# A planner that sets the order of emission counts every result as ready a fixed small reserve later than its clocks say

## The chip, the cores and the metric

One Trainium2 chip, one core. The metric is the device time of one execution in microseconds (us). Most executions of this kernel agree within about 0.3%. Engines: PE (TensorE, matmuls), DVE (VectorE), ACT (ScalarE), POOL (GpSimd), SP (SyncE, here only DMA issue).

## The reference, cut to what matters

T = 512 positions, D = 1024 channels, everything float32.

```python
h = rmsnorm(x, g_mix)
z = h @ w_in                         # conv 2048, q 1024, k 1024, v 1024, gates 2048 columns
y_conv = silu(layernorm(causal_conv_31(a * sigmoid(gate)))) @ w_conv_pw
q, k = partial_rope(q), partial_rope(k)          # 8 heads x 2 parts x 64
# differential attention, causal, per block of 128 queries:
p = softmax(mask(q k^T / 8)); attn = p[part 0] - lam * p[part 1]; o = attn @ v
y_attn = (rmsnorm(o, g_subln) * (1 - lambda_init)) @ w_attn_pw
x = x + (gate_conv * y_conv + gate_attn * y_attn) @ w_out
h2 = rmsnorm(x, g_ffn)
x = x + (silu(h2 @ w_ffn_gate) * (h2 @ w_ffn_up)) @ w_ffn_down     # d_ff = 2816
out = rmsnorm(x, g_final)
```

## The kernel before

**Arithmetic and tiling.** The block is kept transposed, channels on the 128 partitions and the 512 positions along the free axis. Each float32 operand of a dense product is split in a high part (fp32r) and a low rest (fp32r), and a product is three matmuls: high by high, high by low, low by high. Weights come as units of 128x1024 (512 KB each, one DMA on SP's queue into `wr`, 3 buffers). `next_unit` keeps the splitting some units ahead of their use: ACT casts a unit to `wh` (4 buffers), and the rest `wl = wr - wh` (4 buffers) is made on POOL in four pieces of 128x256 for units 3 to 63, on DVE for the others.

**Stages, with their times from the start of the span.** Loading x and its norm, to about 31 us; eight chunks of the convolution branch (`chunkA`, two units and 48 matmuls each), to about 101; eight heads, to about 325 (for each pair of heads `project_v` makes V from two units, then every head has one chunk for q and k); eight chunks of gates, to about 401; four chunks of the attention's output projection, to about 448; then the convolution's projection, `w_out`, the FFN, and a tail, to 908.5.

**Work that is slipped between the dense matmuls.** Generators ("tasks") hold it. `softmaxes(h)` splits q and k of a head (tiles T and `kz`), makes scores (a pair of matmuls for each block of queries and part, called S00, S01, S10, ... here: block, then part), the exponentials and the difference of the two parts. `outputs(h)` transposes that difference (the turns T0, T1, T2: matmuls `at<-ident,T`), splits the result on ACT and DVE, and multiplies it by V (P.V: `at<-T,T`). `head_norm` normalises the heads' outputs during the gate chunks: their reciprocal roots come from one POOL instruction on the tile `oc`. `conv_norm` is the layernorm of the convolution during the attention projection: column sums on PE, a small scaling on DVE (`sm`), a power on POOL (`rc`), four diagonal tiles on DVE (`dg`), a broadcast by PE (`cv<-dg,ones`). `norm_x` and `norm_ffn` have the same shape. The convolution's 31 taps for each channel tile (DVE, `cv<-T,vec_sb,cv`, 248 in all) are filler: `pump` puts one into DVE's queue whenever DVE's planned clock is behind PE's, or before a DVE instruction that would wait. When a channel tile's last tap is emitted, an add onto `csum` (128x512) is put into POOL's queue.

**What sets the order.** Each engine runs its queue in the order of emission, and that order comes from a planner, `class Model` (lines 78 to 125). It keeps a planned clock for each engine (`clk`), and for each tile a planned `ready` time. Every operation recorded (helper line L142, so that nearly all instructions have this line) advances its engine's clock by an assumed cost and sets

```python
for n in outs:
    self.ready[n], self.writer[n] = end + self.LAT[eng] + self.SLACK, eng
```

where LAT is the assumed latency of a hop (PE 0.2, DVE 0.14, ACT 0.145, POOL 0.075, DMA 0.13). `start` takes the latest of the engine's clock and the ready times of what an operation reads and writes, except that PE does not wait for PE. `alloc`, which gives a tile a buffer of its ring, uses the last use of the old tile + 0.13, without SLACK.

`need(tiles)` is the latest ready time of some tiles. A task yields the time that it needs, and is resumed by `service` once that time is due:

```python
def service(until=0.0):
    while True:
        now[0] = max(clk["pe"], until)
        due = [t for t in tasks if t[0] <= now[0]]
```

The dense work calls `service` through `run`, before each three matmuls:

```python
yield need(hi, lo, outs[c], *mov[k])        # chunkA; project_v: need(hi, lo, ps)
```

So `until` is the ready time of what the next dense matmul takes, its own accumulator `outs[c]` among it. That accumulator was last written by PE, with ready time PE's clock + 0.2 + SLACK: a task is thus resumed if it is due within that much of PE's clock.

Of the kernel before, what the change touches and what calls it, by code (L numbers as in the profile page):

```python
# [80 lines left out]
class Model:  # L81


    LAT = {"pe": 0.2, "dve": 0.14, "act": 0.145, "pool": 0.075, "dma": 0.13}
    SLACK = 0.0

    def __init__(self):
        self.clk = {"pe": 0.0, "dve": 0.0, "act": 0.0, "pool": 0.0, "dma": 2.2}
# [21 lines left out]
    def op(self, eng, cost, ins, outs):  # L110
# [5 lines left out]
        for n in outs:  # L116
            self.ready[n], self.writer[n] = end + self.LAT[eng] + self.SLACK, eng

# [945 lines left out]
```

## Time and profile before

| | us |
|---|---|
| runs | 908.42, 910.53, 911.55 (median 910.53) |
| the profiled execution | 910.34 |
| its span | 908.5 (1.84 lie outside the span) |
| PE busy | 886.2 (98% of the span), 4246 matmuls |
| DVE, ACT, POOL busy | 567.8, 373.6, 293.5 |
| chain that ended last | PE 53% and no other engine by 1% |

PE is the engine that never rests for long, so a change can gain only what PE loses in waits. In the rows further below a bracket as `[0.34 <-DVE T L142]` means that the engine stood idle for 0.34 us before this instruction, and that a tile T written by DVE ended the idle time. Matmuls of a row overlap in their pipeline: their starts lie closer than their durations say.

### The profile page before, as it was taken

The page shows a single profiled execution, that of the slowest core. Times are in us where ns is not written, and L with a number is a line of the kernel's source. Part 1 is how long each engine was busy: PE and PEld are TensorE (multiplying, and loading weights), DVE is VectorE, ACT ScalarE, POOL GpSimd, SP SyncE. Part 2 cuts the span into 40 slices and gives each one's busy share as a digit, 9 for nine tenths or more (in the row PEclk, how much of TensorE's full clock was granted, in tenths as well). Part 3 has the DMA queues.
Part 4 walks back from the last instruction along what each step waited for, and adds up shares of the span by engine and source line. Part 5 has one row for each costly group of instructions (what it writes and reads, how often), then busy time and mean ns, then how long its engine had stood idle before and what let it go on. Part 6 is the DMA issues. An engine that isn't in the chain of part 4 may idle for free.

```text
span 908.5 us, 11288 instructions
## 1 busy us (share of the span) xinstructions
PE 886.2 (98%) x4246; PEld 733.1 (81%) x4246; DVE 567.8 (63%) x952; ACT 373.6 (41%) x615; POOL 293.5 (32%) x369
## 2 busy tenths in 40 slices
PE   8989999999999999999999999999999999999996
PEld 6868888888887777688888888888888888888886
DVE  6699899898989889957455553343433433422422
ACT  7332336665657884445322343322232222312212
POOL 2755577683938456455100001111111111000000
PEclk9999999999999999999999999999999999999999
DMA  8222222121121122233323441233332222332302
GB/s 278 93 71 95 91 93 94 48 93 47 66 70 51 70 70 71 78 108 93 105 81 130 147 142 64 76 102 107 100 105 97 93 93 92 116 102 84 116 24 93
DMA packets 26151, 85.20 MB, mean 94 GB/s; under 512 B 3040, under 2 KB 3808, under 8 KB 26096
## 3 DMA queue, kind: packets, MB, share of 16 engines
q1 hardware_dynamic: 24944, 82.52, 27.6%
q10 hardware_dynamic: 1152, 1.97, 0.6%
q8 instruction: 33, 0.54, 0.2%
q14 instruction: 22, 0.18, 0.1%
HBM read 82.38 MB, written 2.10 MB: 93 GB/s over the span
## 4 chain that ended last, share of the span: by engine, by line
PE 53%; DVE 0%; issue 0%; POOL 0%; ACT 0%; POOLq 0%
PE mm L142 27%; PE at L142 22%; PE cv L142 4%; DVE dg L142 0%; DVE T L142 0%; POOL rc L142 0%; ACT T L142 0%; POOLq L196 0%; POOL sm L142 0%; DVE fs L142 0%
## 5 line engine op out<-in xcount | busy, mean ns | idle before, releaser
L142 PE MATMUL mm<-T,wh 128*128 128x512 f32 x1360 | 426.6, 395 | 4.0 <-DVE T L142 3.2
L142 PEld LDWEIGHTS mm<-T,wh 128*128 128x128 f32 x1360 | 251.3, 189 | 58.7 <-DVE T L142 4.2
L142 PE MATMUL mm<-T,wl 128*128 128x512 f32 x680 | 266.2, 391 | 0.5 <-DVE wl L142 0.5
L142 POOL TENSOR_TENSOR wl<-wr,wh 128x256 fp32r<-128x256 f32 x244 | 189.4, 809 | 153.9 <-ACT wh L142 153.9
L142 ACT CAST wh<-wr 128x1024 fp32r<-128x1024 f32 (+1 forms) x148 | 148.9, 1033 | 78.6 <-PE mm L142 38.7
L142 POOL TENSOR_TENSOR T<-T,T 128x256 f32<-128x256 f32 (+1 forms) x96 | 90.1, 949 | 231.0 <-DVE T L142 211.2
L142 DVE SCALAR_TENSOR_TENSOR cv<-T,vec_sb,cv 128x512 f32<-128x512 f32 x232 | 160.7, 747 | 0.1
L142 PE MATMUL at<-T,wh 128*128 128x512 f32 x496 | 154.0, 392 | 0.0
L142 PEld LDWEIGHTS mm<-T,wl 128*128 128x128 f32 x680 | 128.2, 189 | 28.4 <-DVE wl L142 1.0
L142 DVE TENSOR_TENSOR wl<-wr,wh 128x1024 fp32r<-128x1024 f32 (+1 forms) x88 | 101.9, 1186 | 69.8 <-ACT wh L142 69.2
L142 ACT CAST T<-T 128x512 fp32r<-128x512 f32 (+2 forms) x112 | 67.9, 618 | 139.0 <-POOL T L142 85.2
L142 DVE TENSOR_TENSOR T<-T,T 128x512 fp32r<-128x512 f32 (+2 forms) x111 | 86.1, 777 | 58.5 <-ACT T L142 56.6
L142 PEld LDWEIGHTS at<-T,wh 128*128 128x128 f32 x496 | 93.6, 189 | 19.5
L142 DVE TENSOR_TENSOR T<-mm,T 128x512 f32<-128x512 f32 (+1 forms) x76 | 51.8, 683 | 85.1 <-PE mm L142 76.7
L142 PE MATMUL mm<-wh,T 128*128 128x256 f32 (+1 forms) x432 | 101.0, 317 | 0.0
L142 PE MATMUL at<-T,wl 128*128 128x512 f32 x248 | 97.0, 391 | 0.0
L142 ACT ACTIVATE T<-T 128x512 f32<-128x512 f32 (+1 forms) x66 | 40.4, 621 | 122.7 <-DVE T L142 122.6
L142 DVE TENSOR_TENSOR T<-at,T 128x512 f32<-128x512 f32 (+4 forms) x59 | 38.0, 649 | 66.9 <-PE at L142 55.3
L142 ACT ACTIVATE T<-T,sm 128x128 f32<-128x128 f32 (+3 forms) x100 | 56.1, 562 | 53.6 <-DVE sm L142 50.1
L142 PEld LDWEIGHTS mm<-wh,T 128*128 128x128 f32 x432 | 73.1, 190 | 5.4
L142 PE MATMUL mm<-wl,T 128*128 128x256 f32 (+1 forms) x216 | 68.2, 316 | 0.0
L142 PEld LDWEIGHTS at<-T,wl 128*128 128x128 f32 x248 | 46.8, 189 | 9.8
(88 smaller groups left out, 649.2 us busy)
## 6 DMA issues: line engine op xcount, KB each, us to landing
wr<-wall SPq DMA_DIRECT2D x145, 512.0 KB, 3.3
T<-xT SPq DMA_DIRECT2D x16, 256.0 KB, 4.4
out<-T ACTq DMA_DIRECT2D x4, 256.0 KB, 2.8
out<-T SPq DMA_DIRECT2D x4, 256.0 KB, 2.6
wr<-wall SPq DMA_DIRECT2D x4, 128.0 KB, 4.2
T<-cs ACTq DMA_DIRECT2D x2, 256.0 KB, 4.7
T<-gfin SPq DMA_DIRECT2D x2, 256.0 KB, 5.1
T<-mask ACTq DMA_DIRECT2D x1, 256.0 KB, 5.0
```

What stands on the lines that cost most here:

```text
L142: r = f(*args, **kw)
```

## The change

One constant of the planner:

```diff
 class Model:
     LAT = {"pe": 0.2, "dve": 0.14, "act": 0.145, "pool": 0.075, "dma": 0.13}
-    SLACK = 0.0
+    SLACK = 0.15
```

Every operation's results, and every load's (`load` goes through `op`), now count as ready 0.15 us later. The engines' planned clocks move only where an operation is planned to wait. No instruction is added or taken away: 4246 matmuls, 952 DVE, 615 ACT and 369 POOL instructions as before. What changes is the order in each queue, at three places as follows (tile names carry a running number, which differs between the two).

PE, the queue around the first scores of head 3, S00, S01, S10, S11 (`at` tiles from T and `kz`), and a turn of head 2 (`at<-ident,T`); `mm` are dense matmuls. Before (S00 stands nine dense matmuls ahead of the first row):

```order
L142 MATMUL at_2147<-T_386_2060,T_384_2058 128x128
L142 MATMUL at_2147<-kz_157,T_384_2058 128x128
L142 MATMUL at_2164<-T_385_2059,T_383_2057 128x256
L142 MATMUL at_2164<-kz_156,T_383_2057 128x256
L142 MATMUL mm_2111<-wh_1869,T_93_504 128x256
L142 MATMUL mm_2111<-wl_1871,T_93_504 128x256
L142 MATMUL mm_2111<-wh_1869,T_94_506 128x256
L142 MATMUL at_2103<-ident,T_351_1939 128x128
L142 MATMUL at_2103<-ident,T_371_2002 128x128
L142 MATMUL at_2103<-ident,T_351_1939 128x128
L142 MATMUL at_2103<-ident,T_371_2002 128x128
L142 MATMUL mm_2111<-wh_1869,T_98_523 128x256
```

After:

```order
L142 MATMUL at_2222<-T_376_2061,T_374_2059 128x128
L142 MATMUL at_2222<-kz_156,T_374_2059 128x128
L142 MATMUL at_2229<-T_377_2062,T_375_2060 128x128
L142 MATMUL at_2229<-kz_157,T_375_2060 128x128
L142 MATMUL at_2237<-T_376_2061,T_374_2059 128x256
L142 MATMUL at_2237<-kz_156,T_374_2059 128x256
L142 MATMUL at_2220<-ident,T_363_2016 128x128
L142 MATMUL at_2220<-ident,T_380_2083 128x128
L142 MATMUL at_2220<-ident,T_363_2016 128x128
L142 MATMUL at_2220<-ident,T_380_2083 128x128
L142 MATMUL at_2244<-T_377_2062,T_375_2060 128x256
L142 MATMUL at_2244<-kz_157,T_375_2060 128x256
```

The first scores moved from the V projection of heads 4 and 5 (mm of 256 columns) into the q and k chunk behind it; S00, S01, S10 and S11 and the turn now follow each other with no dense matmul between.

POOL, the rests of the two weight units of that same V projection (`wl`, four pieces each), and the rotation of q and k (T 128x256) behind them. Before:

```order
L142 TENSOR_TENSOR wl_1786<-wr_1565,wh_1784 128x256 x4
L142 TENSOR_TENSOR wl_1871<-wr_1687,wh_1869 128x256 x4
L142 TENSOR_TENSOR T_152_916<-T_152_916,T_347_1921 128x512
L142 TENSOR_TENSOR T_346_1920<-T_346_1920,T_2_99 128x256
L142 TENSOR_TENSOR T_348_1925<-T_348_1925,T_346_1920 128x256
```

After:

```order
L142 TENSOR_TENSOR wl_1745<-wr_1561,wh_1743 128x256 x4
L142 TENSOR_TENSOR T_152_916<-T_152_916,T_320_1808 128x512
L142 TENSOR_TENSOR wl_1840<-wr_1612,wh_1838 128x256 x4
L142 TENSOR_TENSOR T_325_1857<-T_325_1857,T_2_99 128x256
L142 TENSOR_TENSOR T_326_1859<-T_326_1859,T_325_1857 128x256
```

The add onto `csum` (128x512) moved from behind the two units to between them.

POOL, the power of `head_norm` (`oc`) among the rests of the gates' weight units. Before:

```order
L142 TENSOR_TENSOR wl_3649<-wr_3505,wh_3647 128x256 x4
L142 TENSOR_TENSOR wl_3712<-wr_3558,wh_3710 128x256 x4
L142 TENSOR_TENSOR wl_3782<-wr_3645,wh_3780 128x256 x4
L142 TENSOR_TENSOR oc_988<-oc_988,mhalf 128x32
L142 TENSOR_TENSOR wl_3848<-wr_3708,wh_3846 128x256 x4
```

After:

```order
L142 TENSOR_TENSOR wl_3798<-wr_3645,wh_3796 128x256 x4
L142 TENSOR_TENSOR wl_3867<-wr_3731,wh_3865 128x256 x4
L142 TENSOR_TENSOR wl_3919<-wr_3794,wh_3917 128x256 x4
L142 TENSOR_TENSOR oc_990<-oc_990,mhalf 128x32
L142 TENSOR_TENSOR wl_3979<-wr_3863,wh_3977 128x256 x4
```

`oc` moved three weight units later in POOL's queue (51 units stand ahead of it, against 48).

## Rows read from the trace of the kernel before

**Rows 1.** Windows: stretch, its us, busy of PE PEld DVE ACT POOL, clock, DMA.

```profile
125.00:350.00 225.00, 217.35 (x1207) 182.86 (x1206) 205.54 (x456) 148.74 (x311) 143.01 (x181) 1.00 0.21 69
400.00:425.00 25.00, 24.64 (x113) 19.96 (x112) 17.81 (x29) 14.48 (x20) 13.73 (x18) 1.00 0.34 104
425.00:900.00 475.00, 475.00 (x2173) 395.30 (x2172) 197.34 (x238) 142.09 (x189) 38.70 (x34) 1.00 0.30 98
```

**Rows 2.** Waits of PE, 125 to 350 us: total us, times, longest.

```profile
PE at L142 <- DVE T L142: 2.7, 8, 0.7
PE at L142 <- DVE kz L142: 2.3, 7, 0.6
PE at L142 <- ACT T L142: 1.6, 4, 0.5
PE at L142 <- DVE sm L142: 1.0, 3, 0.6
```

**Rows 3.** Timeline of PE from 203.2 us: start, us, instruction, [idle before <- releaser].

```profile
203.22 0.28 PE L142 MATMUL mm<-wl,T 128*128 128x256 f32 x1
203.34 0.28 PE L142 MATMUL mm<-wh,T 128*128 128x256 f32 x1
203.96 0.30 PE L142 MATMUL at<-T,T 128*128 128x128 f32 x1 [0.34 <-DVE T L142]
204.59 0.33 PE L142 MATMUL at<-kz,T 128*128 128x128 f32 x1 [0.33 <-DVE kz L142]
```

**Rows 4.** The chain of waits: one chunk of 48 dense matmuls (start, us, what).

```profile
459.19 10.88 PE at L142 x48
```

**Rows 5.** Timeline of PE: the last P.V of the attention.

```profile
322.44 1.04 PE L142 MATMUL at<-T,T 128*128 128x256 f32 x6 [0.36 <-ACT T L142]
```

**Rows 6.** Timeline of DVE, 201.4 to 204.6 us.

```profile
201.44 0.68 DVE L142 TENSOR_TENSOR kz<-T,T 64x512 fp32r<-64x512 f32 x1
202.15 1.67 DVE L142 TENSOR_TENSOR T<-T,T 64x512 fp32r<-64x512 f32 x1
203.84 0.69 DVE L142 TENSOR_TENSOR kz<-T,T 64x512 fp32r<-64x512 f32 x1
```

**Rows 7.** Timeline of POOL, 179 to 206 us.

```profile
184.50 3.11 POOL L142 TENSOR_TENSOR wl<-wr,wh 128x256 fp32r<-128x256 f32 x4 [0.84 <-ACT wh L142]
187.56 7.46 POOL L142 TENSOR_TENSOR T<-T,T 128x512 f32<-128x512 f32 x9
...
201.60 1.66 POOL L142 TENSOR_TENSOR T<-T,T 128x512 f32<-128x512 f32 x1 [0.22 <-DVE T L142]
```

**Rows 8.** Timeline of PE: the second unit of that V projection begins.

```profile
193.49 0.40 PE L142 MATMUL mm<-wh,T 128*128 128x256 f32 x2
```

**Rows 9.** Timeline of POOL, 349 to 372 us: `oc` and two units behind it.

```profile
354.91 5.45 POOL L142 TENSOR_TENSOR oc<-oc,mhalf 128x32 f32<-128x32 f32 x1 [1.39 <-DVE gsub L142]
360.33 5.60 POOL L142 TENSOR_TENSOR wl<-wr,wh 128x256 fp32r<-128x256 f32 x8
```

**Rows 10.** Timeline of POOL, 395 to 450 us.

```profile
398.78 1.29 POOL L142 TENSOR_TENSOR T<-T,T 128x512 f32<-128x512 f32 x1
...
413.20 2.81 POOL L142 TENSOR_TENSOR wl<-wr,wh 128x256 fp32r<-128x256 f32 x4 [1.58 <-ACT wh L142]
415.97 1.02 POOL L142 TENSOR_TENSOR rc<-sm,mhalf 128x4 f32<-128x4 f32 x1
```

**Rows 11.** Timeline of DVE, 410 to 420 us: what `rc` takes, what takes it.

```profile
414.39 0.16 DVE L142 TENSOR_SCALAR sm<-at 128x4 f32<-128x4 f32 x1 [0.77 <-PE at L142]
417.02 2.82 DVE L142 TENSOR_SCALAR dg<-ident,rc 128x128 f32<-128x128 f32 x4 [2.47 <-POOL rc L142]
```

**Rows 12.** Timeline of PE: the broadcast of `conv_norm`.

```profile
419.22 0.49 PE L142 MATMUL cv<-dg,ones 128*128 128x128 f32 x2 [0.17 <-DVE dg L142]
419.90 0.49 PE L142 MATMUL cv<-dg,ones 128*128 128x128 f32 x2 [0.19 <-DVE dg L142]
```

**Rows 13.** Timeline of PE at the start: column sums of `norm_x`, and the wait at 51.12.

```profile
23.26 1.02 PE L142 MATMUL at<-ones,T 128*128 128x1 f32 x8 [1.31 <-DVE T L142]
...
51.12 0.73 PE L142 MATMUL mm<-T,wh 128*128 128x512 f32 x2 [3.25 <-DVE T L142]
```

**Rows 14.** Timeline of DVE: the instruction that releases the wait at 51.12.

```profile
50.42 0.65 DVE L142 TENSOR_TENSOR T<-mm,T 128x512 f32<-128x512 f32 x1
```

## The prediction

> **What bounds the kernel now.** I read the windows first, then the waits of PE, then the timelines of single stretches, and last the queues of the changed kernel. PE is the bound nearly everywhere: from 425 to 900 us it is busy for 475.00 of 475.00 us [rows 1], so nothing is to be had there from any order. What order can touch lies where PE stops: 7.65 us of the 225 from 125 to 350 (heads and the first gate chunks), 0.36 us from 400 to 425, and two waits of the start, 1.31 and 3.25 us [rows 1, 13].
>
> In the attention stretch the list of waits [rows 2] names 22 of them, 7.6 us: on splits by DVE (T, `kz`), on splits by ACT before P.V, on the probabilities before a turn. Each costs more than it shows. Before the scores at 203.96 the bracket says 0.34 us, but dense matmuls of that shape follow each other at 0.12 us (203.22 to 203.34), and here the step is 0.62: 0.50 lost [rows 3]. So 0.16 is to be added to each wait, 22 x 0.16 = 3.5, and about **11 us** are lost: kz 3.4, DVE's T 4.0, ACT's T 2.2, sm 1.5. They are short, 0.34 us shown on average, since the planner lets PE meet an operand when its clocks call it ready, and in fact it is a little late. That is what a reserve of 0.15 us for each hop is aimed at. But DVE is busy for 205.54 of the same 225 us, 91%: PE is the bound with DVE close behind, so the reserve can't be had by making DVE's chains faster, only by putting other PE work ahead of their consumers.
>
> A dense matmul of 512 columns, which is what is put ahead, is worth 10.88 / 48 = 0.227 us, a group of three 0.68 [rows 4].
>
> **The change, part by part.** No instruction comes or goes, so each term is a wait that shrinks or grows. The sum is made on the profiled execution, 910.34 us, which is 0.19 below the median of the runs, 910.53.
>
> *Attention.* A task is resumed if it is due within the ready time of the dense accumulator, and that one grows by the same 0.15 (0.20 to 0.35 ahead of PE's clock). So the reserve of the last hop cancels wherever the dense work asks for its accumulator, and only the earlier hops of a chain (a softmax has DVE, ACT, DVE, ACT, DVE) pile up 0.15 each. The queue shows that this moves things: the first scores of head 3 stand behind what was dense work of the V projection in which they waited, and P.V mostly gets one more group of three matmuls, 0.68 us, between the turn and itself. The wait of P.V is 0.36 + 0.16 = 0.52 at the last head [rows 5], and four of that kind make 2.2; 0.68 us of cover would end them all, and I take half, 1.2, since the cover is not added everywhere. For `kz`, 2.6 of 3.4: the scores are pushed by two or three hops' reserve, against mean losses of 0.49. For DVE's T, 2.2 of 4.0, and for sm, 0.8 of 1.5: half, since in the changed queue S00, S01, S10, S11 and a turn follow each other with no dense matmul between, where nine stood between S00 and S01. A bunch has no cover: if the last of DVE's splits is late for one, PE stands (0.69 us for each split, [rows 6]). Sum **-6.8**, bounds 0 (every wait comes back elsewhere) and -11.
>
> *New waits on weights.* The attention work that moves later leaves PE earlier at the dense work behind it, while POOL's queue keeps its pace. In the V projection of heads 4 and 5 the second unit's rest was ready at 184.50 + 3.11 = 187.61 and PE began it at 193.49: 5.9 us of cover [rows 7, 8]. Counted over PE's queue, 89 attention matmuls stood ahead of that point and now 68; 21 of them at 0.12 to 0.23 us are 3.1 us. The waits that vanish before it take up to 1.6 more, and the add onto `csum` that now stands between the two units is 1.29 us [rows 10]. 5.9 - 3.1 - 1.6 - 1.3 = -0.1: the cover is gone. With POOL's instructions stretching beside DVE's (that add took 1.66 at 201.60, [rows 7]) the wait may be 0 to 3 us; I take 1.5. Two places of the same make, the second unit of the next V projection and the evacuation of the accumulator behind it by ACT, which has the casts in its queue, take 1.0 each by the nearest row, this one. Sum **+3.5**, bounds 0 and 7.
>
> *The heads' roots (`oc`).* 5.45 us on POOL, now behind three more units of 5.60 / 2 = 2.8 us each [rows 9], 8.4 us, while its transposes stand about 60 dense matmuls, 13.6 us, later on PE. The units are needed by the same dense work, so they are not early. The unit behind `oc` gets less cover; 0 to 1.6, I take **+0.3**. The tail of `head_norm` still ends one half chunk ahead of the attention projection.
>
> *The convolution's norm.* `sm` is there at 414.55, but `rc` starts at 415.97, behind a weight unit that ends at 416.01: 1.4 us lost [rows 10, 11]. In the changed queue the column sums stand 18 matmuls later and the broadcast 15, so PE's cover shrinks by 0.68, and `rc` meets the unit done. 1.4 - 0.68 = 0.7 of it stays, as much as the two waits lose (0.17 + 0.19 + 2 x 0.16, [rows 12]). **-0.7**, bounds 0 and -0.7.
>
> *Start, FFN, tail.* Column sums and broadcast of `norm_x` stand three matmuls later, which takes 0.7 off the wait at 23.26. But the wait at 51.12 ends with a DVE instruction at 50.42 whose queue ahead is the same [rows 13, 14]: what is saved before is waited for there. **0**, bounds -0.1 and +0.8. `norm_ffn` moves by two groups and stays covered by its chunk (10.88). The convolution's taps have their last `csum` add at 398.78 + 1.29 [rows 10], not near what waits for it. Zero.
>
> Sum: -6.8 + 3.5 + 0.3 - 0.7 = -3.7, so 906.6 on the profiled run and 906.8 on the median. I forecast **907 us**, since of the unknown places the new waits are the ones that I could see least of.
>
> **What speaks against the change in the profile.** The wait at 203.96 is no short lateness of a hop. DVE's split before it took 1.67 us, its neighbours of the same shape 0.68 and 0.69; from 201.60 to 203.26 POOL ran its 128x512 add, and DVE's instruction ended 0.56 later [rows 6, 7]: it seems to have begun when POOL's ended. Such a delay is 1 us, not 0.15, and it sits where the two engines meet, which any new order shuffles. The Trainium skill, page "SBUF — State Buffer", section "Who interferes with whom", says that a DVE instruction with two SBUF inputs contends with a GpSimd instruction that reads SBUF, and that whoever issues first holds the shared ports for its whole instruction while the other fully blocks. The trace agrees at this place (1.67 against 0.68). By that rule alone the attention term would be 0 and not -6.8.
>
> **The rivals.**
>
> *The reserve does not reach the lateness (same).* What PE waits for is DVE blocked by POOL, or DVE's own 91% load, and both shift with the order. Then the 11 us come back in other places: attention 0 to -3, new waits +1 to +3, the norm -0.7: 908 to 912, middle 910. For it: the 1.67 us of rows 6, the bunched scores, and the cancelling of the last hop. Against it: the means of the four groups of waits are 0.33 to 0.40 us, not 1. That the change does nothing because the reserve cancels is in this case as well; the queues show that it does move things.
>
> *The weights become late (slower).* The mechanism of the +3.5, at its upper end: PE arrives at a unit of V before POOL is done, and the whole dense stream stands, since nothing else is in PE's queue. Place: second units of the V projections, and the unit behind `oc`. Price: up to 3 us at each of two V places and the evacuation, 9, plus 1.6 for `oc`, against a gain that is then nearer 5: 910.5 + 10.6 - 5.7 = 915.4 at the far end, 914 as its middle. It decides once the new waits exceed the gain by 2.7 us. For it: the cover of 5.9 us is used up by 3.1 + 1.6 + 1.3. Against: a third of these 6.0 us is itself a gain that must first be made.
>
> *More than forecast (faster).* New waits stay under 1 us, attention gives 9 of its 11: 901 to 903. Against it is the bunching.
>
> **How the numbers follow.** A measurement of this kernel tells about 0.3%, 2.7 us, from no change. Chances: forecast (904 to 908) 0.40, more than that 0.12, same 0.30, slower 0.18. Of the forecast's 0.40, 0.38 lies below 907.8, and 0.02 above. So faster by over 0.3% has 0.38 + 0.12 = 0.50, within 0.3% 0.30 + 0.02 = 0.32, slower 0.18. The range leaves out the deeper half of "more" and the upper half of "slower": **902 to 914**. The faster part's own range is 902 to 907.8.
>
> **What would show it.** Right: between 125 and 350 us the waits of PE on `kz` and on DVE's T fall from 5.0 us to about 2, those on ACT's T to under 1; the list of waits gains a line of `mm` on POOL's `wl` in the second unit of the V projections, of 1 to 3 us; `rc` starts within 0.3 us of `sm`; 51.12 moves by less than 0.3 while the wait before it grows to about 3.9. From 425 on the windows stay at full busy time. Wrong: waits of the attention of 6 us or more with new names (the rival "same"), `wl` waits above 6 us together (slower), or a changed clock anywhere, of which I took none.

## The result, and the profile after

The changed kernel takes 903.60 us in the median of four runs (901.14 to 904.27) against 910.47 of the kernel before: a ratio of 0.9922, 95% interval 0.9896 to 0.9949. It is faster by 6.9 us, where 3.5 was forecast with a range of 902 to 914. The profiled execution took 904.26 us with a span of 902.5; that of before 910.34 and 908.5.

The windows (columns as in [rows 1]) and the waits of PE from 125 to 350 us of the changed kernel, which answer to [rows 1, 2]:

```profile
125.00:350.00 225.00, 219.79 (x1235) 188.59 (x1234) 208.84 (x462) 148.51 (x311) 146.97 (x190) 1.00 0.22 73
...
400.00:425.00 25.00, 24.98 (x118) 20.70 (x117) 20.20 (x32) 15.52 (x22) 14.50 (x17) 1.00 0.26 85
425.00:890.00 465.00, 465.00 (x2119) 386.67 (x2118) 192.30 (x230) 138.03 (x182) 34.81 (x30) 1.00 0.30 99
```

```profile
PE at L142 <- DVE T L142: 1.5, 2, 0.8
PE at L142 <- DVE sm L142: 1.3, 3, 0.6
PE mm L142 <- ACT T L142: 1.2, 1, 1.2
PE at L142 <- ACT T L142: 0.6, 1, 0.6
PE at L142 <- DVE kz L142: 0.6, 1, 0.6
```

PE stands for 5.2 us of the stretch in place of 7.65, and in the same 225 us does 1235 matmuls in place of 1207. Of 22 waits 8 are left, one of them new: a dense matmul (`mm`) on ACT. Measured from start to start of neighbouring matmuls, less what the same pair takes undisturbed, the attention's waits above 0.12 us were 12.5 us before and are 5.7 after, the new one, 1.39, apart.

Where the 6.0 us of span went follows from the start times of the same dense matmul in both traces (after less before): +0.60 at the 97th (36 us), +0.61 when the first attention work begins, -5.67 at the last of the gate chunks (400 us), -6.30 behind the convolution's norm, -6.35 at the end of PE's work; the tail gives 0.34 back. So the stretch with the heads gave 6.3, the norm 0.6, and the start cost 0.6.

The norm is as forecast. Timelines of POOL, DVE and PE, which answer to [rows 10 to 12]:

```profile
413.10 1.02 POOL L142 TENSOR_TENSOR rc<-sm,mhalf 128x4 f32<-128x4 f32 x1 [3.98 <-DVE sm L142]
```

```profile
414.15 2.82 DVE L142 TENSOR_SCALAR dg<-ident,rc 128x128 f32<-128x128 f32 x4 [1.13 <-POOL rc L142]
```

```profile
416.18 1.34 PE L142 MATMUL cv<-dg,ones 128*128 128x128 f32 x8
```

`rc` starts 0.08 us behind `sm` (412.86 + 0.16 = 413.02), no weight unit is in its way, and the broadcast runs in one piece with no bracket.

### The profile page after: what moved, and what is told of

Read it like the earlier page. It is cut to its first block, busy times and chain, and to the rows that moved or that the text cites. A ratio compares the mean times of both kernels' runs of the same rounds, so it can differ in the third digit from the quotient of the medians.

```text
span 902.5 us, 11283 instructions
## 1 busy us (share of the span) xinstructions
PE 882.8 (98%) x4246; PEld 733.1 (81%) x4246; DVE 567.2 (63%) x952; ACT 373.1 (41%) x615; POOL 292.1 (32%) x369
## 4 chain that ended last, share of the span: by engine, by line
PE 83%; DVE 11%; ACT 2%; issue 2%; DMA 1%; POOL 1%; POOLq 0%; SPq 0%; ACTq 0%
PE mm L142 52%; PE at L142 27%; DVE T L142 7%; PE cv L142 4%; DVE cv L142 2%; ACT T L142 2%; DVE kz L142 1%; POOL wl L142 1%; DMA wr<-wall 1%; DMA T<-xT 0%; DVE dg L142 0%; DVE sm L142 0%; ACT L142 0%; DVE wl L142 0%; POOL rc L142 0%
## 5 line engine op out<-in xcount | busy, mean ns | idle before, releaser
L142 POOL TENSOR_TENSOR wl<-wr,wh 128x256 fp32r<-128x256 f32 x244 | 186.7, 800 | 134.8 <-ACT wh L142 118.6
```

Source lines behind the costliest of these rows:

```text
L142: r = f(*args, **kw)
```

## Experiments

**Where the gain is made.** Two kernels share the edit between them. `heads_only`:

```diff
+            model.SLACK = 0.15
             for h in range(NH):
...
+            model.SLACK = 0.0
             spawn(head_norm())
```

> The reserve of 0.15 only while the eight heads are emitted (set when the first V projection is emitted, back to 0 when the norm of the heads is put in the list of tasks). Theory (the gain is made in the attention, by consumers that stand behind more dense matmuls): the queue is that of the change from there to head 3 and close to it behind, so 904 to 905 us: the attention's -6.3 of the changed kernel, without the -0.6 of the convolution's norm and without the +0.6 of the start. Rival (the gain is a sum of lucky places all over the program): 907 to 909. The wait at 51.12 us is back where it was in the kernel before, since the start has its old order.

Measured: 905.94 us, ratio 0.9952 (0.994 to 0.9964). `all_but_heads` has 0.15 everywhere else:

> The complement: the reserve everywhere except while the heads are emitted. Theory: attention waits as in the kernel before up to head 6 (the first seven heads' work stands at the same dense matmul), the start +0.6, the convolution's norm -0.6 to -0.7, and at the last head, whose P.V gets three more matmuls, up to -1: 909.5 to 910.5 us, no difference that can be told. Rival (gain all over): 907 or less.

Measured: 906.61 us, ratio 0.9958 (0.9946 to 0.997). The first is somewhat short of its forecast, the second far better, -3.5 for -0.5, and that looks like the rival. The start times of the dense matmuls say otherwise. In `all_but_heads` the heads are as before up to the 1151st dense matmul (it begins 0.56 us later, the 767th 0.57), then 2.75 us go between that one and the 1535th, and 0.66 at the norm. The tasks of heads 6 and 7 are still running when the last head has been emitted, and the queue with the reserve back on moves the last head's first turn from the 1239th to the 1275th dense matmul: its waits (0.52, 0.56, 0.87, 0.52 at heads 6 and 7 before) are gone. In `heads_only` the attention gives 4.3 and the norm nothing. The gain is in the attention's waits and the norm's; what was wrong is where the edit's line cuts the work.

**Which hop's reserve counts.** `pe_only` and `not_pe` add the reserve to PE's results alone, or to all others:

```diff
-            self.ready[n], self.writer[n] = end + self.LAT[eng] + self.SLACK, eng
+            self.ready[n], self.writer[n] = end + self.LAT[eng] + (self.SLACK if eng == "pe" else 0.0), eng
```

> The reserve on PE's results alone: look-ahead and PE hops grow together. Theory: the two cancel, the attention's work stands at the same dense matmuls as before for all heads but parts of 2 and 3, so 910 to 911 us, the waits of the attention as in the kernel before (7.6 us shown). Rival (the longer look-ahead is itself what helps, or hurts): 907 or 913.

Measured: 912.73 us, ratio 1.0025 (1.0015 to 1.0035). That is the rival's time (913). The attention's work stands as forecast where it stood before, but against the kernel before 1.0 us is lost at 186.3 and 2.6 us at 206.6, in heads 2 and 3. Timelines of PE, ACT, DVE and POOL there:

```profile
186.26 0.33 PE L142 MATMUL at<-kz,T 128*128 128x128 f32 x1 [1.29 <-DVE kz L142]
...
206.60 0.58 PE L142 MATMUL at<-T,T 128*128 128x256 f32 x1 [2.61 <-ACT T L142]
```

```profile
205.57 0.72 ACT L142 ACTIVATE T<-T,sm 128x512 f32<-128x512 f32 x1 [5.04 <-DVE sm L142]
206.20 0.35 ACT L142 COPY T<-at 128x256 f32<-128x256 f32 x1
```

```profile
184.55 1.65 DVE L142 TENSOR_TENSOR kz<-T,T 64x512 fp32r<-64x512 f32 x1
...
201.34 1.12 DVE L142 TENSOR_TENSOR T<-T,T 64x512 fp32r<-64x512 f32 x1
202.49 1.12 DVE L142 TENSOR_TENSOR kz<-T,T 64x512 fp32r<-64x512 f32 x1
203.65 1.51 DVE L142 SCALAR_TENSOR_TENSOR T<-T,sm,T 128x384 f32<-128x384 f32 x1
```

```profile
196.09 6.97 POOL L142 TENSOR_TENSOR wl<-wr,wh 128x256 fp32r<-128x256 f32 x8
203.03 1.71 POOL L142 TENSOR_TENSOR T<-T,T 128x512 f32<-128x512 f32 x1
```

At 186.26 PE waits for a split of 1.65 us that runs beside POOL's add onto `csum` (183.94 to 185.66). At 206.60 PE wants the next of the score buffers (`at`, three of them), and the one due is emptied by an ACT copy that stands behind a scaling which waits for DVE, whose splits take 1.12 us and not 0.69 beside POOL's weight pieces, and whose next instruction takes 1.51 us beside POOL's add (0.61 elsewhere). Nothing is late by a hop; a queue blocks in order. So alone, the longer look-ahead brings nothing. That it hurts by itself is not shown: the loss lies where DVE and POOL meet.

> The reserve on all results but those of PE, so that the accumulator's ready time, and with it the look-ahead of the tasks, stays at 0.20 and cancels nothing. Theory: the reserve now counts at the last hop too, most attention work stands 3 to 30 dense matmuls later than in the changed kernel; the waits of PE in the attention fall below the changed kernel's 5.7 us (start to start), to 2 to 4, and the time to 900 to 903 us, unless weights or accumulators come late by more than 2 us. Rival (what is left are DVE's blocked instructions and DVE's load, which no reserve of this size reaches): 903 to 905, same waits under other names.

Measured: 904.96 us, ratio 0.9938 (0.9925 to 0.9951). Up to the 1151st dense matmul this kernel is 13.7 us ahead of the one before (the changed kernel: 9.4; the two have put off different amounts of attention work, so that is no gain yet), and then one wait takes 5.2. So the time is the rival's (903 to 905), by one wait and not by many under other names. Timelines of PE, ACT and DVE:

```profile
291.74 0.58 PE L142 MATMUL at<-T,T 128*128 128x256 f32 x1 [5.17 <-DVE sm L142]
```

```profile
286.00 3.55 ACT L142 CAST T<-T 64x512 fp32r<-64x512 f32 x6
```

```profile
289.94 0.69 DVE L142 TENSOR_TENSOR T<-T,T 64x512 fp32r<-64x512 f32 x1
290.66 0.69 DVE L142 TENSOR_TENSOR kz<-T,T 64x512 fp32r<-64x512 f32 x1
291.38 0.29 DVE L142 CUSTOM_DVE_ANT_0 T<-at,T 128x128 f32<-128x128 f32 x1
```

DVE empties head 6's score buffer at 291.38, behind head 7's four splits, which wait for six casts on ACT. That reading was tried. `not_pe_h7` holds the splits of head 7, and no other, back until head 6's softmax is through:

```diff
-                while started[0] < h - 2:
+                while started[0] < h - (1 if h == 7 else 2):
```

> The kernel with the reserve on all but PE's results, and for head 7 alone the splits of q and k are put into the queues only when head 6's softmax is through (one line). Theory: the one wait of 5.4 us in that kernel (scores of head 6 on the score buffers, which DVE reads behind head 7's four splits, which stand behind six casts on ACT) vanishes, and with it the half clock that followed it (11 dense matmuls at 0.20 more each): 904.96 - 5.4 - 2.2 = 897 to 899 us. Rival (PE would have waited there for its buffers anyhow, or the splits are late for head 7 now): 902 to 906.

Measured: **899.65 us**, ratio 0.9878 (0.9865 to 0.9892), which beats both kernels. By the profiled spans 7.0 us go (904.8 to 897.8) of the 7.6 expected, by the medians 5.3; 0.7 of the 7.0 lie already at the start, ahead of the heads. The wait is gone; waits of PE from 125 to 350 us:

```profile
PE at L142 <- DVE sm L142: 1.3, 4, 0.4
PE at L142 <- DVE kz L142: 1.1, 2, 0.6
PE at L142 <- DVE T L142: 0.7, 1, 0.7
```

Two controls show what that line is worth by itself.

> The kernel before with the one line of not_pe_h7 alone (head 7's splits queued only after head 6's softmax), no reserve. Theory (that line is worth something only where a reserve has pushed head 6's scores behind head 7's splits): 910 to 911 us, no change, or a little slower since head 7 starts later. Rival (the line is the gain, the reserve little): 906 or less.

Measured: 909.82 us, ratio 0.9994 (0.9985 to 1.0003).

> The changed kernel with that line. Its only long wait in the attention is 1.39 us (start to start) of a gate chunk at 299.3 us, on an accumulator that ACT empties behind a scaling of head 7's softmax. Theory: the line moves that softmax, so the wait may go: 902 to 904 us; what not_pe_h7 has gained beyond is the reserve at the last hop. Rival (the line is what made not_pe_h7 fast): 900 or less.

Measured: 902.42 us, ratio 0.992 (0.9907 to 0.9933). With no reserve it is worth nothing, in the changed kernel the 1.39 us wait goes but the time is not told apart from the change's own, and only with the reserve at the last hop does it give 5.3 (904.96 to 899.65).

**How much.** Four other values of the one constant.

> SLACK = -0.15 in place of 0.0: the same edit with the other sign. Theory (waits of PE in the attention come from consumers that are a hop's lateness too early): most attention work stands 3 to 30 dense matmuls earlier than before, so the 12 us of waits (start to start) grow by 3 to 6: 913 to 917 us. Rival (any new order is as good as any other, the old one had bad luck): 904 to 911.

Measured: 927.23 us, ratio 1.0186 (1.0172 to 1.02). The sign is right and the size three times the forecast. Waits of PE, 125 to 350 us:

```profile
PE at L142 <- ACT T L142: 11.9, 14, 2.0
PE at L142 <- DVE T L142: 5.3, 9, 1.1
PE at L142 <- DVE kz L142: 2.0, 5, 0.6
```

The attention's waits are 28.5 us from start to start, 16.0 more than before, nearly all of the loss. A new order alone is no gain: this one is as new as the other. The norm's 0.6 is no matter of the sign, though. It is gained here too (+16.98 at the last of the gate chunks, +16.36 behind the norm), with `rc` 1.75 us behind `sm`: its four `dg` take 0.88 us in place of 2.82, with no weight unit beside them on POOL.

> SLACK = 0.075. The queue of PE is already much like the changed kernel's (attention work 3 to 60 dense matmuls later than before). Theory: half of the reserve, most waits gone already where they are shorter than two or three hops' 0.075, some left: 904 to 907 us. Rival (a reserve must be the size of the lateness, 0.3 to 0.5 us a wait): 908 to 910.

Measured: 906.19 us, ratio 0.9965 (0.9953 to 0.9977), as forecast.

> SLACK = 0.20. The last P.V of head 7 stands behind 1383 dense matmuls (1281 before, 1335 in the changed kernel, 1422 with 0.35). Theory: the norm of the heads still has its cover from the gate chunks, which it lost with 0.35, so no wait on oc; the attention's short waits as small as in the changed kernel: 900 to 905 us, unless a queue blocks in order for some us as in not_pe. Rival (the cover ends just above 0.15): 910 or more, with waits on oc.

Measured: 903.58 us, ratio 0.9933 (0.9922 to 0.9945), as forecast.

> SLACK = 0.35. Theory: attention work moves a further 4 to 45 dense matmuls later; the short waits (0.3 to 0.9 us) mostly vanish, sum of the attention's waits 2 to 4 us start to start, 900 to 903 us. Rival (what is left after 0.15 are queues that block in order, at two or three places of 1 to 5 us that no reserve sees): 903 to 907, the long waits as many as in the changed kernel or more.

Measured: 936.29 us, ratio 1.0279 (1.0265 to 1.0293): neither theory nor rival. Timelines of POOL and PE, and the window (columns as in [rows 1]):

```profile
405.05 5.45 POOL L142 TENSOR_TENSOR oc<-oc,mhalf 128x32 f32<-128x32 f32 x1 [4.13 <-DVE gsub L142]
```

```profile
410.56 1.02 PE L142 MATMUL at<-ident,oc 128*8 128x128 f32 x4 [4.92 <-POOL oc L142]
412.76 3.78 PE L142 MATMUL at<-T,T 8*128 8x512 f32 x8 [1.18 <-ACT T L142]
```

```profile
400.00:430.00 30.00, 21.10 (x65) 13.36 (x64) 12.02 (x20) 8.17 (x14) 6.38 (x3) 0.66 0.06 21
```

The heads' work is now so late that their norm runs out of gate chunks. `oc`'s transposes stand behind the last of the 1536 dense matmuls ahead of the attention projection (1395 before, 1455 in the changed kernel, 1509 with 0.20), and the rest of the norm runs with nothing beside it, at a granted clock of 0.66 in the mean. From the 1535th to the 1583rd dense matmul 20.5 us are lost; the attention itself lost 6.5. With 0.20 there is no wait on `oc` in the trace. So the constant has a slope on the left, the same time at 0.15 and 0.20 (903.60 and 903.58), and an edge between 0.20 and 0.35; where in there was not tried.

**DVE held by POOL.** `no_csum` leaves out POOL's adds onto `csum` from the third channel tile on, so the sum from which the layernorm takes its mean is that of two tiles; the planner still counts them:

```diff
-                                G.tensor_tensor(out=csum[0], in0=csum[0], in1=done[-1], op=ALU.add)
+                                model.op("pool", 0.05 + T * 0.0023, [csum[0].tensor.name, done[-1].tensor.name],
+                                         [csum[0].tensor.name])
```

> The kernel before with POOL's adds onto the sum of the convolution's channels left out from the third channel tile on (six instructions of 128x512); the planner still counts them, so that every queue keeps its order. Theory that DVE was held by POOL at 202.15 us: that DVE split takes 0.7 and not 1.67, the two waits behind it (203.96 and 204.59, 1.06 start to start) vanish or halve: 909 to 909.8 us, and the rest of the attention keeps its waits. Rival (the 1.67 us have another cause): the split stays at 1.6 or more and the time at 910.1.

Measured: 909.16 us, ratio 0.9983 (0.9974 to 0.9992). DVE's timeline, which answers to [rows 6]:

```profile
201.34 0.68 DVE L142 TENSOR_TENSOR kz<-T,T 64x512 fp32r<-64x512 f32 x1
202.05 0.69 DVE L142 TENSOR_TENSOR T<-T,T 64x512 fp32r<-64x512 f32 x1
202.77 0.69 DVE L142 TENSOR_TENSOR kz<-T,T 64x512 fp32r<-64x512 f32 x1
```

The split takes 0.69 in place of 1.67, and the two waits behind it (1.06 us from start to start) are gone. The theory holds: here DVE was held by POOL's add. The rule that the prediction quoted from the Trainium skill, page "SBUF — State Buffer", section "Who interferes with whom", agrees with this place: 1.67 us beside the add, 0.69 without it.

## Why the prediction was right, point by point

**Bound and place: right.** From 425 to 890 us PE is busy throughout in the changed kernel as well, and all that moved lies in the attention, the norm and the start.

**Attention, -6.8: as found from start to start (12.5 to 5.7).** By the groups, which come to -6.0, with 0.16 added to each wait: `kz` 3.4 to 0.8 (2.6 forecast, 2.6 found), DVE's T 4.0 to 1.8 (2.2 and 2.2), ACT's T 2.2 to 0.8 (1.2 and 1.4), sm 1.5 to 1.8 (0.8 forecast, nothing found). That the sum agrees to the tenth is luck: of three of the four groups the prediction took about half, as an estimate, and one of these came to nothing. The mechanism is shown by the runs with the other sign and with parts of the reserve: consumers that stand behind more dense matmuls. That the last hop's reserve is cancelled by the look-ahead is shown too: PE's reserve alone moves almost nothing, and without it the tasks stand later still.

**New waits, +3.5: the term that was mis-sized.** Found: +1.4, and at none of the three places named. The second unit of that V projection (the first row POOL's, the second PE's, which answer to [rows 7, 8]; the unit begins with the second matmul of PE's row):

```profile
186.37 2.83 POOL L142 TENSOR_TENSOR wl<-wr,wh 128x256 fp32r<-128x256 f32 x4 [4.36 <-DVE sm L142]
```

```profile
188.80 0.40 PE L142 MATMUL mm<-wh,T 128*128 128x256 f32 x2
```

POOL has the unit done at 189.20, PE begins it at 188.9 and does not wait. The cover did fall from 5.9 us to below zero, as worked out, -0.3 for -0.1 (by the traces 107 attention matmuls stood ahead of that point and now 84, 23 fewer, where the prediction counted 21). But the unit is made in four pieces of 0.71 us and used piece by piece, three matmuls of 0.12 us to each: the first was there at about 187.1, the third at 188.5, where PE takes it at 189.6. The cover had to be counted for each piece, and the price of a cover just gone is then nothing. The one new wait stands in a gate chunk. PE and ACT:

```profile
299.33 0.74 PE L142 MATMUL mm<-T,wh 128*128 128x512 f32 x2 [1.23 <-ACT T L142]
```

```profile
296.87 0.40 ACT L142 ACTIVATE T<-T,sm 128x128 f32<-128x128 f32 x1 [2.31 <-DVE sm L142]
297.29 1.28 ACT L142 ACT_TABLE_LOAD   x1
298.59 0.69 ACT L142 ACTIVATE T<-mm,vec_sb 128x512 f32<-128x512 f32 x1
```

ACT empties the accumulator behind a scaling of the last head that waits 2.31 us for DVE, and a table load. The kind was named (ACT has other work ahead of the evacuation), the place was not.

**`oc`, +0.3: nothing.** It starts at 361.52, right behind a weight unit, and ends at 366.98; its transposes come at 369.46 without a wait. The term had the right mechanism, though: it is the edge that `s_35` fell over, and its price there was 20 us and not the 1.6 of the upper bound, since not a weight unit is late then but the whole rest of the norm stands bare.

**Start, 0: +0.6 in the profiled execution, and not by the order.** The windows with the granted clock (columns as in [rows 1]) of the kernel before, of the changed kernel, and of `after_h7`, which has the same queues up to head 7:

```profile
24.60:27.80 3.20, 3.20 (x9) 2.47 (x8) 0.00 (x0) 0.00 (x0) 3.20 (x5) 0.50 0.52 169
31.60:34.80 3.20, 3.20 (x16) 2.63 (x14) 0.69 (x1) 2.48 (x3) 0.61 (x1) 1.00 0.48 164
```

```profile
24.60:27.80 3.20, 3.20 (x16) 2.63 (x14) 0.00 (x0) 0.00 (x0) 3.20 (x5) 1.00 0.50 164
31.60:34.80 3.20, 3.20 (x9) 2.52 (x8) 0.69 (x1) 2.15 (x3) 0.94 (x1) 0.50 0.45 160
```

```profile
24.60:27.80 3.20, 3.20 (x16) 2.62 (x15) 0.00 (x0) 0.00 (x0) 3.20 (x5) 1.00 0.51 165
31.60:34.80 3.20, 3.20 (x15) 2.63 (x14) 0.69 (x1) 2.25 (x3) 0.85 (x1) 1.00 0.45 164
```

At a granted clock of 0.50 (1.2 of 2.4 GHz) PE does 9 matmuls in 3.2 us, at 1.00 15 or 16. In the kernel before the half clock lies under the chain of `norm_x`, where PE has time to spare (the changed kernel, at the full clock there, waits 0.51 and three times 0.19 before the broadcast); in the changed kernel behind that chain, where it has none; in `after_h7` at neither place. The 97th dense matmul begins at 36.76 in the one and at 35.27 in the other: 1.5 us between two executions of the same start. The forecast that the wait at 51.12 would take up what is saved at 23.26 was wrong for this run: that wait stayed at 3.2, and the work ahead of it came later with PE. The prediction named a changed clock anywhere as a sign of being wrong: it is one for this term, and not for the attention, where the clock stays at 1.00.

**Total.** -6.8 + 1.4 and a remainder of -0.9 (steps under 0.12 us, many of them behind each wait) are the -6.3 of the heads; -0.6 for the norm, +0.6 at the start and +0.34 in the tail make -6.0 by the spans. The forecast of -3.7 was short by nearly what the new waits were over-sized. The range held with 1.6 us to spare: one of the four runs, 901.14, lies below it.

**The rivals.** "Same" rested on a true mechanism, DVE held by POOL, and `no_csum` prices POOL's adds onto `csum` at 1 to 1.3 us, not 11. What POOL's weight pieces cost in the same way was not tried by itself (in `no_csum` too, splits beside them take 1.1 to 1.3 us). By the rival DVE stays as slow and the waits come back elsewhere. Groups of DVE's splits, 125 to 350 us (count, then total us and mean ns), first the kernel before, then the changed one:

```profile
L142 DVE TENSOR_TENSOR T<-T,T 64x512 fp32r<-64x512 f32 x16 | 15.5, 969 | 0.8 <-ACT T L142 0.3
L142 DVE TENSOR_TENSOR kz<-T,T 64x512 fp32r<-64x512 f32 x16 | 14.6, 911 | 0.5
```

```profile
L142 DVE TENSOR_TENSOR T<-T,T 64x512 fp32r<-64x512 f32 x16 | 15.4, 960 | 1.3 <-ACT T L142 0.9
L142 DVE TENSOR_TENSOR kz<-T,T 64x512 fp32r<-64x512 f32 x16 | 13.5, 843 | 0.3
```

DVE did stay nearly as slow, and the attention's waits still fell to less than half. At the place of 203.96 the split still takes 1.69 us in the changed kernel, and PE isn't there any more. "Slower" came true with the same edit at 0.35.

## What to carry to other kernels

A schedule that plans to meet each operand just in time loses a little at every meeting; where the engine that bounds has independent work to put in between, a small reserve on each result can save much of that (here 6.9 us, with no instruction added), and a reserve below zero tells whether the sign is right. It pays until some later chain runs out of the work that covers it, so look for that edge (here between 0.20 and 0.35) before the constant is raised. What no reserve tried here removes are waits of several us behind a queue blocked in order: they are found one by one in the timelines, and one line against one of them, in `not_pe`, gave 5 us.

## What the runs showed of the hardware

After PE had stood for some us (2.5 in `s_20`, 2.6 in `pe_only`, 5.2 in `not_pe`), its granted clock fell to half, and dense matmuls (of 512 columns, in `not_pe`) went on at 0.43 us in place of 0.227. In `not_pe`, behind the wait of 5.17 us (window, columns as in [rows 1]):

```profile
291.70:297.00 5.30, 5.26 (x13) 4.23 (x14) 4.96 (x11) 4.17 (x9) 0.00 (x0) 0.50 0.01 3
```

Eleven matmuls lost 0.20 each, so a wait of 5.2 us cost 7.4. In the changed kernel the waits of the attention, none above 1.23 us, left the clock at 1.00. The length of a single wait does not tell which: in `s_m15` a wait of 1.72 us left it at 1.00, in `s_35` it fell behind one of 1.45 us, and in `s_20` it fell once more at 394.4 us, where no wait had been above 0.51 us but the matmuls of the heads' norm (8 rows) had stood between the dense ones. At the start the half clock fell at one place in some executions, at two in others, of kernels with the same order there; the four runs of the changed kernel, 901.14 to 904.27 us, had mean clocks of 0.998 (901.14), 0.996 (902.93), 0.994 (904.26) and 0.995 (904.27).
